# Copying the state-space input out of PSUM in pairs, in another piece order, and turning the second half of a finished block one piece later

## The chip, the cores and the metric

The kernel runs on one core of one Trainium2 chip. The time is the device time of one execution in microseconds. Beside the timed runs there is one profiled execution, whose trace gives every instruction's start and duration.

## The reference

One decoder layer over 256 tokens of width 2048: a SwiGLU feed-forward, a mixer (differential attention beside a state-space branch, S5), and a second SwiGLU feed-forward. Each is fed by an input `u` that is shifted and scaled by a conditioning vector, and each result passes a layer norm. Cut to what matters here:

```
mod = silu(c) @ w_cond + b_cond                       # 9 rows of 2048: shift, scale, gate for three sub-layers
h   = (silu(u @ w1) * (u @ w3)) @ w2                  # feed-forward, inner width 5632
q, k, v, s = split(u @ w_in)                          # mixer: 1024 columns each
attn = diff_attention(q, k, v);  ssm = s5(s)          # s5 scans s over the 256 tokens in 64 groups of 16 channels
h   = concat(attn, ssm) @ w_out
x   = layer_norm(alpha * x + weight * (1 + gate) * h) # after each sub-layer
```

## The kernel before, in words

All weights are read once, as **pieces** of 128 x 1024 numbers (512 KB). `Stream` runs one job for each piece, in the order of a list that Python builds. Around each job it does four things: SP loads the piece into a `raw` buffer, ScalarE casts it to a rounded `hi` (L691), VectorE subtracts to get the rest `lo`, and TensorE multiplies the input (itself split into `Uh` and `Ul`) with `hi` and `lo`. The cast and the subtraction are issued four pieces ahead of the multiplication (`AHEAD`). VectorE also does the conditioning product (`gv`) in between, at places that are fixed when the program is built. Each engine executes its instructions in the order in which the Python code issues them, so the list of jobs and the calls after each job set everything. `stream.later(n, f)` runs `f` after the job that is n pieces later. Nearly every vector and matrix instruction carries line L106, that of a helper, so the rows are told apart by tile names.

**The mixer's s pieces.** `mk_s(t, hf)` multiplies one piece of `w_in`. There are eight tiles `t` of 128 columns of s, and two halves `hf` of the 2048-long sum. Before, the list is all eight tiles with the first half, then all eight with the second. Two neighbouring tiles (t even, t odd) share one PSUM bank (tile `ps`), each using 256 of its 512 columns. After a tile's second half `post` copies its columns to `sT` with ScalarE (L1147) and stores that to a DRAM buffer `sD` by a DMA that ScalarE issues (L1150). After tiles 3 and 7 POOL issues four loads each (L1156) that read `sD` back in the layout of the scan, into `U4` (`U` in the profile). The first matmuls of the scan (`enter` in `s5_batch`, on `U` and `s5e`) stand ahead of job 17 of the mixer, that is behind the sixteen s pieces and one q piece. They need the four loads of tiles 0 to 3.

During the first five s pieces the second half of the mixer's input is still being made: after each of jobs 1 to 4 TensorE turns blocks of `Y`, and ScalarE and VectorE make `Uh` and `Ul` of them. The pieces with hf = 1 need those.

**The k-outer blocks of the feed-forward.** The first blocks of `w1` and `w3` are multiplied in several passes over parts of the inner sum (`mk_ko`). Each block b has two parts, m = 0 (`w1`) and m = 1 (`w3`), and each part holds two PSUM banks. Between passes the partial sums are kept in the SBUF tile `kosum`. In the last pass of the first feed-forward a part is two pieces, so that a block is four. After a part's last piece VectorE adds both banks to `kosum`, which frees the banks. After m = 1, one piece later, `up_post` multiplies silu of the one with the other, and `turn_up` puts two **turnings** on the list: two pieces later TensorE transposes half of the product into one PSUM bank (`ps<-ident,kosum`), ScalarE casts it to `Hh` (L1010) and VectorE makes `Hl`, which frees that bank; one piece after that comes the other half. Four banks are held all through by a block that stays in PSUM, so that only four change hands here. The silu of the next block's m = 0 (L990) falls beside the first turning.

In the second feed-forward, where a part of the last pass is four pieces, the same code runs with b = 1 to 3 (b = 0 takes another path).

Of the kernel before, what the change touches and what calls it, by code (L numbers as in the profile page):

```python
# [17 lines left out]
T = 256  # L18
# [99 lines left out]
def tile_layer(tc, A, out):  # L118
    nc = tc.nc
    V, S, PE, SP, GP = Meter(nc.vector), nc.scalar, Meter(nc.tensor), nc.sync, nc.gpsimd  # L120
    with ExitStack() as ctx:
# [8 lines left out]
        def psum():  # L130
            return psp.tile([128, 512], F32, tag="ps", name="ps")
# [4 lines left out]
        def small(shape, name, bufs=2, dt=F32, tag=None):  # L136
            return tmp.tile(shape, dt, tag=tag or name, name=name, bufs=bufs)

        def w1(shape, name):
            return small(shape, name, 5, tag="w1")  # L140
# [49 lines left out]
        for q in range(4):  # L190
            p, cs = psum(), slice(q % 2 * 512, q % 2 * 512 + 512)
# [9 lines left out]
        sD = dram.tile([1024, 4, 64], F32, tag="sD", name="sD")  # L201
# [530 lines left out]
        stream = Stream()  # L732
# [19 lines left out]
        def between(k):  # L752

            if k in mid:
                mid.pop(k)()
# [22 lines left out]
        def form_b(pd, hi, lo, AH, AL, k0, first, last):  # L778
            for t, p in enumerate(pd):
                if isinstance(p, tuple):  # L780
                    for i in range(2):
                        form_b1(p[i], hi, lo, AH, AL, k0, t, first, last, 256 * i, 256 * i + 256)
                else:
                    form_b1(p, hi, lo, AH, AL, k0, t, first, last)
# [27 lines left out]
        def halves(w, h):  # L812
            return w[:, h * CH:(h + 1) * CH]
# [112 lines left out]
        def ffn(w13, wd, blk, passes, tiles, kept):  # L926
            jobs = []
            B = {}

            def mk_ko(i, b, m, kp):  # L930

                k0, k1 = passes[i]
                keep = 4 * b in kept
                n = len(passes) - 1
                first = i == 0 or not (keep or b == order(i)[0])
                last = i == n or not (keep or b == order(i)[-1])

                def mm(hi, lo):
                    if first and 2 * kp == k0:
                        B["ko", b, m] = [psum(), psum()]  # L940
                    form_b(B["ko", b, m], hi, lo, *st["U"], 2 * kp, first and 2 * kp == k0, last and 2 * kp + 2 == k1)

                def post():
                    if keep or not last:
                        return
                    ps = B.pop(("ko", b, m))
                    if i == n and ("sum", b) not in B:
                        if m == 0:
                            B["s", b] = gated(ps)
                        else:  # L950
                            up_post(B.pop(("s", b)), ps, 4 * b)
                        return
                    if m == 0 and ("sum", b) not in B:
                        B["sum", b] = (pslab if b in ((1, 2) if blk else (3, 4)) else slab)("kosum")
                    a = [B["sum", b][:, (2 * m + t) * 512:(2 * m + t + 1) * 512] for t in range(2)]
                    for t in range(2):
                        if ("added", b, m) not in B:
                            S.copy(a[t], ps[t])
                        else:
                            V.tensor_tensor(a[t], ps[t], a[t], op=ALU.add)  # L960
                    B["added", b, m] = True
                    if i < n:
                        return
                    if m == 0:
                        B["a", b] = a
                        stream.later(1, lambda: gated(a, a))
                        return
                    s = B.pop(("a", b))
                    if b < 4:
                        stream.later(1, lambda: up_post(s, a, 4 * b))  # L970
                    else:
                        stream.later(1, lambda: hold(b, s, a))
                return Job(mm, halves(w13[b, m, kp // 2], kp % 2), post if 2 * kp + 2 == k1 else None)

            def order(i):

                bs = [b for b in range(tiles // 4) if 4 * b not in kept]
                return bs if (len(passes) - 1 - i) % 2 == 0 else bs[::-1]

            def hold(b, s, ps):  # L980

                B["held", b] = [w2([128, 512], "sg") for _ in range(2)]
                for t in range(2):
                    V.tensor_tensor(B["held", b][t], s[t], ps[t], op=ALU.mult)

            def gated(ps, s=None):

                s = s or [w2([128, 512], "sg") for _ in range(2)]
                for t in range(2):
                    S.activation(s[t], ps[t], AF.Silu)  # L990
                return s

            def up_post(s, ps, slot):

                for t in range(2):
                    V.tensor_tensor(s[t], s[t], ps[t], op=ALU.mult)
                turn_up(s, slot)

            def turn_up(s, slot, n=2):
                if slot == 0:  # L1000
                    st["H"] = pairs("H")

                def turned(i):
                    p = psum()
                    for j in range(2):
                        for t in range(2):
                            PE.transpose(p[:, j * T + t * 128:j * T + t * 128 + 128],
                                         s[t][:, (2 * i + j) * 128:(2 * i + j + 1) * 128], ident)
                    hh, hl = (kx(x, slot + 2 * i, 0, 2 * T) for x in st["H"])
                    S.copy(hh, p)  # L1010
                    V.tensor_tensor(hl, p, hh.bitcast(F32), op=ALU.subtract)
                stream.later(n, lambda: turned(0))
                stream.later(n + 1, lambda: turned(1))

            def mk_up(b, m, kp, slot):
                def mm(hi, lo):
# [69 lines left out]
            for i, (k0, k1) in enumerate(passes):  # L1086
                n = len(jobs)
                kps = range(k0 // 2, k1 // 2)
                bs = order(i) + [x // 4 for x in kept[::4]]
                c = (0 if i else 1 if blk else 2)  # L1090
# [4 lines left out]
            for pi, (f0, nf) in enumerate(PIECES):  # L1095
                n = len(jobs)
                for s in range(max(0, min(tiles - f0, nf)), nf, 4):
                    jobs += [mk_up((f0 + s) // 4, m, kp, s) for m in range(2) for kp in range(8)]
                if pi == 1:
                    for s in range(0, tiles - f0, 4):  # L1100
                        b = 4 + s // 4
# [15 lines left out]
        def mixer():  # L1117
            jobs = []
            M = {}
# [10 lines left out]
            def mk_s(t, hf):  # L1130
                def mm(hi, lo):
                    if hf == 0 and t % 2 == 0:
                        M["ps", t // 2] = psum()
                    M["pt"] = p = M["ps", t // 2][:, (t % 2) * T:(t % 2 + 1) * T]
                    for k in range(8):
                        between(8 * hf + k)
                        w = hi[:, k * 128:(k + 1) * 128]
                        PE.matmul(p, w, kx(st["U"][0], 8 * hf + k), start=hf == 0 and k == 0 and t % 2 == 0,
                                  stop=False, skip_group_check=True)
                        PE.matmul(p, w, kx(st["U"][1], 8 * hf + k), start=False, stop=False, skip_group_check=True)  # L1140
                    for k in range(8):
                        PE.matmul(p, lo[:, k * 128:(k + 1) * 128], kx(st["U"][0], 8 * hf + k), start=False,
                                  stop=hf == 1 and k == 7, skip_group_check=True)

                def post():
                    s = w1([128, 4, 64], "sT")
                    S.copy(s, M["pt"].rearrange("p (c i) -> p i c", i=4))  # L1147
                    if t % 2:
                        M.pop(("ps", t // 2))
                    S.dma_start(sD[t * 128:(t + 1) * 128], s)  # L1150
                    if t % 4 == 3:
                        h = t // 4
                        if h == 0:
                            M["U4"] = slab("U4")
                        for i in range(4):
                            GP.dma_start(  # L1156
                                M["U4"][32 * i:32 * i + 32, h * 1024:(h + 1) * 1024]
                                .rearrange("p (g c) -> p g c", c=64),
                                sD[h * 512:(h + 1) * 512, i, :].rearrange("(g p) c -> p g c", p=32))
                return Job(mm, halves(A["win_a"][t], hf), post if hf else None)  # L1160
# [300 lines left out]

            g08 = small([128, 1], "g08", 1)
            V.tensor_scalar(g08, sublng, 1.0 - LAMBDA_INIT, None, op0=ALU.mult)
            jobs += [mk_s(t, hf) for hf in range(2) for t in range(8)]
            for h in range(NH):
                jobs += [mk_qk(h, w, hf) for w in "qk" for hf in range(2)]
            jobs += [mk_v(db, c) for db in range(2) for c in range(8)]
# [79 lines left out]
        for i in range(4 * NT1):  # L1547
            n = ((10, 12, 16, 16)[i] if i < 4 else NS + math.ceil((i - 3) * NS / (GA[0] - 3)) if i <= GA[0] else
                 min(4 * NS, 2 * NS + math.ceil((i - GA[0]) * NS / GA[1])))
# [129 lines left out]
```

## Time and profile before

| what | value |
|---|---|
| timed runs, median of 3 (lowest, highest) | 1914.42 us (1912.57, 1918.12) |
| profiled execution, its own time | 1912.22 us |
| its span, first to last instruction | 1910.4 us |
| mean granted TensorE clock | 0.989 |
| HBM traffic | 278 GB/s over the span |

About 1.8 us lie around the span. Times below count from the span's start. "Idle" before a TensorE instruction, with the name of what released it, is time that TensorE lost; idle of another engine costs nothing by itself.

### The profile page before, as it was taken

Reading aid. Unit: us, or ns where it says so; the run is one execution under the profiler, and the core shown is the slowest. Engines: PE = TensorE matmul, PEld = TensorE weight load, DVE = VectorE, ACT = ScalarE, POOL = GpSimd, SP = SyncE. Lnnn points to the kernel's source line nnn. Section 1 sums busy time; section 2 is a strip of 40 time slices with the busy share of each in tenths; the row PEclk is TensorE's granted clock in tenths of the full one; section 3 lists DMA queues with packets and bytes.
Section 4 is the critical chain, followed back from the end, with each engine's and each line's share of the span. In section 5 each row is a group of like instructions: output and inputs, shape, how many; then the busy total and the mean of one; then the engine's idle time right before and its main releaser. Section 6 shows DMA issues by size and latency. Waiting matters only on the chain.

```text
span 1910.4 us, 25429 instructions
## 1 busy us (share of the span) xinstructions
PE 1858.5 (97%) x9326; PEld 1567.5 (82%) x9326; DVE 1488.1 (78%) x2255; ACT 889.4 (47%) x1211; POOL 65.0 (3%) x119
## 2 busy tenths in 40 slices
PE   6999999999999999899999998999999999999996
PEld 5888878888888888889999886888888888888885
DVE  6889899978888979888998987887876555445468
ACT  3544444465445433634457635544444444344442
POOL 0000000000000000111210000000000000000000
PEclk9999999999999999999999998999999999999998
DMA  9999878889899888798988885998887555565563
GB/s 375 363 338 315 296 247 292 295 306 309 305 347 326 308 323 312 280 337 294 313 268 311 283 309 202 339 357 275 294 279 249 187 188 191 194 215 187 191 233 110
DMA packets 151935, 532.36 MB, mean 279 GB/s; under 512 B 21841, under 2 KB 23297, under 8 KB 150657
## 3 DMA queue, kind: packets, MB, share of 16 engines
q1 hardware_dynamic: 137234, 495.32, 74.3%
q0 software_dynamic: 6512, 23.89, 3.7%
q10 hardware_dynamic: 8064, 11.54, 1.7%
q8 instruction: 73, 1.20, 0.2%
q14 instruction: 52, 0.43, 0.1%
HBM read 513.34 MB, written 17.33 MB: 278 GB/s over the span
## 4 chain that ended last, share of the span: by engine, by line
PE 87%; DVE 6%; DMA 4%; ACT 2%; issue 1%; POOL 0%; SPq 0%; DVEq 0%; ACTq 0%; POOLq 0%
PE ps L106 87%; DVE lo L106 2%; DVE Y L106 2%; DMA raw<-in_f1w_dram 1%; DVE gv L106 1%; ACT hi L691 1%; DMA early<-in_w_cond_dram 1%; DMA raw<-in_wout_dram 0%; DMA U<-sD 0%; DVE st L106 0%; DVE r L106 0%; DMA sD<-sT 0%; DMA early<-in_wc_dram 0%; ACT Y L865 0%; DVE early L106 0%
## 5 line engine op out<-in xcount | busy, mean ns | idle before, releaser
L106 DVE TENSOR_TENSOR lo<-raw,hi 128x1024 fp32r<-128x1024 f32 x630 | 766.3, 1222 | 342.1 <-ACT hi L691 338.5
L691 ACT CAST hi<-raw 128x1024 fp32r<-128x1024 f32 x630 | 661.4, 1053 | 705.8 <-PE ps L106 461.0
L106 PE MATMUL ps<-hi,Uh 128*128 128x512 f32 x1472 | 583.7, 397 | 16.7 <-ACT Uh L318 9.7
L106 PE MATMUL ps<-hi,Ul 128*128 128x512 f32 x1472 | 577.5, 392 | 0.8 <-DVE Ul L106 0.8
L106 PE MATMUL ps<-lo,Uh 128*128 128x512 f32 x1472 | 457.4, 392 | 1.3 <-DVE lo L106 1.3
L106 PEld LDWEIGHTS ps<-hi,Uh 128*128 128x128 f32 x1472 | 278.7, 189 | 77.8 <-ACT Uh L318 10.4
L106 PEld LDWEIGHTS ps<-lo,Uh 128*128 128x128 f32 x1472 | 278.4, 189 | 60.9 <-DVE lo L106 2.0
L106 PEld LDWEIGHTS ps<-hi,Ul 128*128 128x128 f32 x1472 | 279.0, 190 | 58.1 <-DVE Ul L106 1.9
L106 DVE SCALAR_TENSOR_TENSOR gv<-gv,sc 128x1024 f32<-128x1024 f32 x258 | 314.2, 1219 | 1.4 <-DMA gv<-in_w_cond_dram 1.3
L106 PE MATMUL ps<-hi,Hh 128*128 128x512 f32 (+1 forms) x716 | 274.6, 385 | 0.0
L106 PE MATMUL ps<-hi,Hl 128*128 128x512 f32 (+1 forms) x716 | 273.6, 383 | 0.0
L106 PE MATMUL ps<-lo,Hh 128*128 128x512 f32 (+1 forms) x716 | 216.5, 384 | 1.8 <-DVE lo L106 1.8
L106 PEld LDWEIGHTS ps<-lo,Hh 128*128 128x128 f32 x716 | 133.0, 188 | 29.1 <-DVE lo L106 2.6
L106 PEld LDWEIGHTS ps<-hi,Hh 128*128 128x128 f32 x716 | 134.5, 188 | 26.8 <-issue 0.4
L106 PEld LDWEIGHTS ps<-hi,Hl 128*128 128x128 f32 x716 | 134.6, 188 | 26.0
L106 PE MATMUL ps<-Uh,hi 128*128 128x256 f32 x384 | 97.9, 292 | 2.4 <-ACT sT L1147 1.8
L106 PE MATMUL ps<-Ul,hi 128*128 128x256 f32 x384 | 95.7, 286 | 0.1
L106 PEld LDWEIGHTS ps<-Uh,hi 128*128 128x128 f32 x384 | 74.2, 193 | 6.2 <-ACT sT L1147 2.7
L106 PEld LDWEIGHTS ps<-Ul,hi 128*128 128x128 f32 x384 | 74.2, 193 | 0.8 <-DVE Ul L106 0.7
L1010 ACT CAST Hh<-ps 128x512 fp32r<-128x512 f32 x44 | 25.8, 587 | 78.6 <-PE ps L106 78.6
L106 PE MATMUL ps<-Uh,lo 128*128 128x256 f32 x384 | 53.9, 283 | 0.0
L106 DVE TENSOR_TENSOR Hl<-ps,Hh 128x512 fp32r<-128x512 f32 x44 | 30.3, 688 | 30.0 <-ACT Hh L1010 29.7
(229 smaller groups left out, 1393.4 us busy)
## 6 DMA issues: line engine op xcount, KB each, us to landing
raw<-in_f1w_dram SPq DMA_DIRECT2D x264, 512.0 KB, 6.0
raw<-in_f2w_dram SPq DMA_DIRECT2D x264, 512.0 KB, 4.7
gv<-in_w_cond_dram SPq DMA_DIRECT2D x258, 512.0 KB, 7.1
raw<-in_win_a_dram SPq DMA_DIRECT2D x48, 512.0 KB, 6.0
raw<-in_wout_dram SPq DMA_DIRECT2D x32, 512.0 KB, 5.8
early<-in_w_cond_dram SPq DMA_DIRECT2D x28, 512.0 KB, 7.6
s5m<-scrB POOLq DMA_DIRECT2D x8, 1024.0 KB, 8.4
raw<-in_win_v_dram SPq DMA_DIRECT2D x16, 512.0 KB, 4.8
```

What stands on the lines that cost most here:

```text
L106: return f(*a, **k)
L691: S.copy(hi, raw)
L1010: S.copy(hh, p)
```

## The change

It has two parts.

**The s pieces.** The list of jobs becomes tiles 0 to 5 with the first half, tiles 0 to 3 with the second, tiles 6 and 7 with the first, tiles 4 to 7 with the second. An even tile's `post` does nothing; the odd tile's `post` copies both halves of the bank and stores both. The number of copies (8), stores (8) and loads (8) is the same. The loads of tiles 0 to 3 are issued after job 9 where it was job 11, those of tiles 4 to 7 after job 15 as before.

**The second turning.** For b below 3 on the path through `kosum` the second turning runs two pieces after the first, where it was one. That is three blocks of the first feed-forward (b = 0, 1, 2) and two of the second (b = 1, 2).

```
-                        stream.later(1, lambda: up_post(s, a, 4 * b))
+                        stream.later(1, lambda: up_post(s, a, 4 * b, 2 if b < 3 else 1))
...
-            def turn_up(s, slot, n=2):
+            def turn_up(s, slot, n=2, step=1):
...
                 stream.later(n, lambda: turned(0))
-                stream.later(n + 1, lambda: turned(1))
+                stream.later(n + step, lambda: turned(1))
...
                 def post():
-                    s = w1([128, 4, 64], "sT")
-                    S.copy(s, M["pt"].rearrange("p (c i) -> p i c", i=4))
-                    if t % 2:
-                        M.pop(("ps", t // 2))
-                    S.dma_start(sD[t * 128:(t + 1) * 128], s)
+                    if t % 2 == 0:
+                        return
+                    p = M.pop(("ps", t // 2))
+                    for i in range(2):
+                        s = w1([128, 4, 64], "sT")
+                        S.copy(s, p[:, i * T:(i + 1) * T].rearrange("p (c i) -> p i c", i=4))
+                        S.dma_start(sD[(t - 1 + i) * 128:(t + i) * 128], s)
...
-            jobs += [mk_s(t, hf) for hf in range(2) for t in range(8)]
+            jobs += [mk_s(t, hf) for ts, hf in (((0, 1, 2, 3, 4, 5), 0), ((0, 1, 2, 3), 1), ((6, 7), 0), ((4, 5, 6, 7), 1))
+                     for t in ts]
```

On ScalarE, at the mixer's s pieces, this stood in a row before (`ps_6793` is the bank of tiles 0 and 1, `ps_6930` that of tiles 2 and 3; the cast `hi` is that of the piece four ahead):

```order
L1147 COPY sT_7203<-ps_6793 128x256
L1150 DMA sD_128<-sT_7203 128x256
L691 CAST hi_7207<-raw_7063 128x1024
L1147 COPY sT_7246<-ps_6793 128x256
L1150 DMA sD_128<-sT_7246 128x256
L691 CAST hi_7250<-raw_7099 128x1024
L1147 COPY sT_7283<-ps_6930 128x256
L1150 DMA sD_128<-sT_7283 128x256
```

And now:

```order
L1151 COPY sT_7159<-ps_6793 128x256
L1152 DMA sD_128<-sT_7159 128x256
L1151 COPY sT_7162<-ps_6793 128x256
L1152 DMA sD_128<-sT_7162 128x256
L691 CAST hi_7166<-raw_7015 128x1024
L691 CAST hi_7209<-raw_7063 128x1024
L1151 COPY sT_7248<-ps_6930 128x256
L1152 DMA sD_128<-sT_7248 128x256
L1151 COPY sT_7251<-ps_6930 128x256
L1152 DMA sD_128<-sT_7251 128x256
```

Copies and stores come two by two, with two casts between the pairs, and the first pair stands two casts earlier than the second copy of its bank did. On TensorE the piece that follows a pair writes another bank than the one that is being copied, where before the odd tile's piece wrote the bank that the even tile's copy was reading.

On VectorE, in the last pass of the first feed-forward, this stood in a row before (`kosum_856` is block 0, `kosum_584` block 1, `kosum_481` block 2; `ps_2040` and `ps_2041` are block 1's banks for m = 1, `ps_2087` the second turning of block 0, `ps_2103` and `ps_2104` block 2's banks for m = 0):

```order
L106 TENSOR_TENSOR kosum_584<-ps_2040,kosum_584 128x512
L106 TENSOR_TENSOR kosum_584<-ps_2041,kosum_584 128x512
L106 TENSOR_TENSOR Hl_2012<-ps_2087,Hh_2010 128x512
L106 TENSOR_TENSOR lo_2095<-raw_1989,hi_2094 128x1024
L106 SCALAR_TENSOR_TENSOR gv_1944,acc_1892<-gv_1944,sc_74 128x1024
L106 TENSOR_TENSOR kosum_584<-kosum_584 128x512 x2
L106 TENSOR_TENSOR lo_2120<-raw_2018,hi_2119 128x1024
L106 TENSOR_TENSOR kosum_481<-ps_2103,kosum_481 128x512
```

And now (`ps_2110` is the second turning, `ps_2096` and `ps_2097` are block 2's banks):

```order
L106 TENSOR_TENSOR kosum_584<-ps_2040,kosum_584 128x512
L106 TENSOR_TENSOR kosum_584<-ps_2041,kosum_584 128x512
L106 TENSOR_TENSOR lo_2088<-raw_1989,hi_2087 128x1024
L106 SCALAR_TENSOR_TENSOR gv_1944,acc_1892<-gv_1944,sc_74 128x1024
L106 TENSOR_TENSOR Hl_2012<-ps_2110,Hh_2010 128x512
L106 TENSOR_TENSOR kosum_584<-kosum_584 128x512 x2
L106 TENSOR_TENSOR lo_2120<-raw_2018,hi_2119 128x1024
L106 TENSOR_TENSOR kosum_481<-ps_2096,kosum_481 128x512
```

`Hl` of the second turning moves behind one `lo` and one `gv`; nothing else on VectorE moves. On TensorE the four transposes of the second turning move behind the first piece of block 2. By the program's waits, block 2's second bank was the one that the add `kosum_584<-ps_2040` frees; now the second turning takes that bank, and block 2's first piece takes the bank of the first turning and one that the adds of block 1's m = 0 freed.

More of the change, by code (lines that the diff above doesn't have):

```diff
@@ L991, in gated, with up_post @@
                 return s
-            def up_post(s, ps, slot):
+            def up_post(s, ps, slot, step=1):
                 for t in range(2):
                     V.tensor_tensor(s[t], s[t], ps[t], op=ALU.mult)
-                turn_up(s, slot)
-            def turn_up(s, slot, n=2):
+                turn_up(s, slot, 2, step)
+            def turn_up(s, slot, n=2, step=1):
                 if slot == 0:
@@ L1133, in mm @@
                         M["ps", t // 2] = psum()
-                    M["pt"] = p = M["ps", t // 2][:, (t % 2) * T:(t % 2 + 1) * T]
+                    p = M["ps", t // 2][:, (t % 2) * T:(t % 2 + 1) * T]
                     for k in range(8):
```

## The prediction

> **What bounds the kernel now.** First the profile's page: the busy line and the chain that ended last.
>
> ```profile
> PE 1858.5 (97%) x9326; PEld 1567.5 (82%) x9326; DVE 1488.1 (78%) x2255; ACT 889.4 (47%) x1211; POOL 65.0 (3%) x119
> ...
> PE 87%; DVE 6%; DMA 4%; ACT 2%; issue 1%; POOL 0%; SPq 0%; DVEq 0%; ACTq 0%; POOLq 0%
> ```
>
> TensorE (PE) is busy for 97% of the span and holds 87% of the chain. The change takes away no matmul, so it can only win back time in which PE waits. The waits of PE alone, longest first in total (total us, times, longest), name three that lie where the change works:
>
> ```profile
> PE ps L106 <- DVE kosum L106: 3.3, 3, 1.2
> ...
> PE ps L106 <- DMA U<-sD: 2.3, 1, 2.3
> PE ps L106 <- ACT sT L1147: 1.8, 4, 0.5
> ```
>
> Together 7.4 us; the other waits of PE lie elsewhere. Whether time won there reaches the end is read from stretches behind the first and the second place (stretch, its length, then busy us of PE, PEld, DVE, ACT, POOL, granted clock, DMA share, GB/s):
>
> ```profile
> 400.00:460.00 60.00, 60.00 (x315) 49.29 (x318) 48.62 (x73) 33.26 (x59) 3.65 (x6) 1.00 0.88 308
> ...
> 850.00:900.00 50.00, 50.00 (x425) 48.80 (x425) 38.77 (x69) 20.67 (x41) 9.72 (x17) 1.00 0.91 297
> ```
>
> PE is busy without a gap there while VectorE (DVE) has 11 of 60 and 11 of 50 us free. Loads, casts and subtractions follow PE's own progress, since their buffers come free by it. So what PE wins stays won. About 0.3% (5.7 us) is what a measurement of this kernel can tell from no change.
>
> **The copies of s.** ScalarE (ACT) in order of time at the s pieces with hf = 1 (start, duration, what, idle before it); the eight copies run from 820.68 to 843.73:
>
> ```profile
> 820.68 0.37 ACT L1147 COPY sT<-ps 128x256 f32<-128x256 f32 x1 [2.78 <-PE ps L106]
> 821.08 0.33 ACTq L1150 DMA_DIRECT2D sD<-sT  x1
> 821.51 1.06 ACT L691 CAST hi<-raw 128x1024 fp32r<-128x1024 f32 x1 [0.45 <-ACT sT L1147]
> 824.29 0.37 ACT L1147 COPY sT<-ps 128x256 f32<-128x256 f32 x1 [1.72 <-PE ps L106]
> ...
> 827.16 0.37 ACT L1147 COPY sT<-ps 128x256 f32<-128x256 f32 x1 [1.00 <-PE ps L106]
> ...
> 831.17 0.33 ACTq L1150 DMA_DIRECT2D sD<-sT  x1
> ...
> 843.73 0.37 ACT L1147 COPY sT<-ps 128x256 f32<-128x256 f32 x1 [1.73 <-PE ps L106]
> ```
>
> And PE, on the first of four such places:
>
> ```profile
> 821.11 0.39 PE L106 MATMUL ps<-Uh,hi 128*128 128x256 f32 x1 [0.46 <-ACT sT L1147]
> ```
>
> A copy starts when its piece ends. From an even tile's copy to the odd tile's are 3.61 us (820.68 to 824.29), from odd to even 2.87 (824.29 to 827.16). A piece takes 2.87, and the odd tile's piece is held up until the even tile's copy has left the shared bank: 0.74 us, of which 0.46 show as idle and the rest is the last matmul running out. Four times 0.74 is **2.96 us**. After the change no piece follows a copy of its own bank: the next one writes the next pair's. The copies, 2 x 0.83 us with their stores (820.68 to 821.51), then lie beside a piece of 2.87. The cast behind them comes up to 0.83 later, but it is for a piece four ahead, some 11 us; without that cover 4 x 0.83 would fall on PE. I take the whole 2.96. The four waits are the bound above. A bound below zero would need the second half of the input, which job 6 now asks for, to be late:
>
> ```profile
> 810.91 0.76 DVE L106 TENSOR_TENSOR Ul<-uf,Uh 128x256 fp32r<-128x256 f32 x2
> ```
>
> It is complete at 811.67. Job 6 starts 3 pieces before the first copy (820.68 - 3 x 2.87 = 812.07) and uses its last block later still. Nothing waits.
>
> **The scan's input.** PE's one wait for U, and POOL's loads of tiles 0 to 3:
>
> ```profile
> 848.87 1.97 PE L106 MATMUL ps<-U,s5e 128*128 128x64 f32 x16 [2.30 <-DMA U<-sD]
> ```
>
> ```profile
> 838.16 2.59 POOL L1156 DMA_DIRECT2D U<-sD  x4 [46.89 <-ACT sT L1147]
> ```
>
> From tile 3's store (831.17) to the loads' issue are 6.99 us, from there to PE's start 10.71. Tile 3's piece becomes the tenth of the list; in the old trace the tenth ended at 824.29, less one hold-up 823.55. Tile 2's copy and store (0.83) go first, then tile 3's copy, so its store starts at 823.55 + 0.83 + 0.40 = 824.78. Then 824.78 + 6.99 + 10.71 = 842.48. PE is ready at 848.87 - 2.30 - 2.96 = 843.61. U is 1.1 us early and the wait goes: **2.30 us**. The spread of the store and the loads (us to landing, least, median, most) gives the other bound:
>
> ```profile
> DMA to landing us min/median/max: 4.4/6.9/8.9
> ```
>
> ```profile
> DMA to landing us min/median/max: 6.5/7.7/8.6
> ```
>
> With the slowest of each, 2.0 and 0.9 over the median, U comes 1.8 us after PE, and 0.5 us is won.
>
> [...]
>
> **The second turning.** PE in the last pass of the first feed-forward; `ident,kosum` are the turnings:
>
> ```profile
> 251.11 0.60 PE L106 MATMUL ps<-ident,kosum 128*128 128x128 f32 x4
> ...
> 254.28 0.51 PE L106 MATMUL ps<-hi,Uh 128*128 128x512 f32 x1 [1.18 <-DVE kosum L106]
> ...
> 258.50 0.39 PE L106 MATMUL ps<-hi,Uh 128*128 128x512 f32 x1
> ...
> 261.23 0.60 PE L106 MATMUL ps<-ident,kosum 128*128 128x128 f32 x4
> ...
> 264.42 0.60 PE L106 MATMUL ps<-ident,kosum 128*128 128x128 f32 x4
> ...
> 267.49 0.50 PE L106 MATMUL ps<-hi,Uh 128*128 128x512 f32 x1 [1.08 <-DVE kosum L106]
> ```
>
> A piece is 2.73 (258.50 to 261.23), a turning with the piece behind it 3.19 (261.23 to 264.42). A lap of four pieces and two turnings would be 2 x 3.19 + 2 x 2.73 = 11.84. It is 13.21:
>
> ```profile
> 254.28:267.49 13.21, 12.13 (x56) 9.72 (x57) 11.80 (x17) 6.22 (x8) 0.00 (x0) 1.00 0.67 237
> ```
>
> So each of three laps loses 1.37, on the bank that an add frees late. DVE is nearly as full, 11.80 of 13.21. Its rows:
>
> ```profile
> 253.54 1.28 DVE L106 TENSOR_TENSOR kosum<-ps,kosum 128x512 f32<-128x512 f32 x2
> ...
> 259.95 1.28 DVE L106 TENSOR_TENSOR kosum<-ps,kosum 128x512 f32<-128x512 f32 x2
> ...
> 264.46 1.23 DVE L106 TENSOR_TENSOR lo<-raw,hi 128x1024 fp32r<-128x1024 f32 x1 [1.29 <-ACT hi L691]
> 265.60 1.22 DVE L106 SCALAR_TENSOR_TENSOR gv<-gv,sc 128x1024 f32<-128x1024 f32 x1
> 266.75 0.08 DVE L106 DVE_READ_ACCUMULATOR gv<-gv,sc 128x1 f32 x1
> 266.75 1.28 DVE L106 TENSOR_TENSOR kosum<-ps,kosum 128x512 f32<-128x512 f32 x2
> 267.95 0.68 DVE L106 TENSOR_TENSOR Hl<-ps,Hh 128x512 fp32r<-128x512 f32 x1
> ```
>
> Count from the first turning (261.23). The add starts at +5.52 (266.75) and its first half frees the bank at +6.25: before it DVE idles for a cast that ACT makes behind `Hh` and silu of this same turning, so the add hangs on the turning and not on the queue. After the change PE does turning and piece (+3.19), then block 2's first piece at once (+5.92), and only then asks for that bank: a wait of 0.33 where 1.37 was lost. But from that add to the next block's first add DVE works 6.41 without a gap (253.54 to 259.95), and the next first turning needs a bank of that one: +5.52 + 6.41 + 0.73 = +12.66. PE would be there at +6.25 + 3.19 + 2.73 = +12.17. So the lap becomes 12.66 and no shorter, 0.54 less than 13.20 (DVE's idle 1.29 shrinks to 0.75, so the add still hangs on the turning). Three laps: **1.62 us**. Bounds: 3 x 1.37 = 4.1 if neither wait appears; nothing if DVE fills the lap again; a loss is the last rival below. I take 1.62, since both waits follow from rows of this stretch.
>
> In the second feed-forward PE does not wait at these places. Rows of PE, DVE and SP there:
>
> ```profile
> 1353.07 0.60 PE L106 MATMUL ps<-ident,kosum 128*128 128x128 f32 x4
> ```
>
> ```profile
> 1353.20 1.28 DVE L106 TENSOR_TENSOR kosum<-ps,kosum 128x512 f32<-128x512 f32 x2
> ```
>
> ```profile
> 1362.67 0.42 SPq L880 DMA_DIRECT2D bb<-in_lnb_dram  x1
> ```
>
> The second turning moves one piece, to 1355.8; the add has freed a bank by then, 1353.9. SP's load of `bb` takes over the slab that this turning reads, and SP's weight loads stand behind it, but it is issued 7 us later. Zero, either way.
>
> **The sum.** 2.96 + 2.30 + 1.62 = 6.88. The profiled execution took 1912.22, so it would take 1905.3. The median of the runs shown is 1914.42, 2.2 above it; the median is what is compared, so I predict 1914.42 - 6.88 = 1907.5.
>
> **The rivals.**
> - *The laps lose nothing any more* (-4.1 there, 9.4 in all: 1905.1). For it: DVE can work only 11.80 in a lap. Against: the two bank waits above.
> - *The laps win nothing*: DVE stays the bound and the wait only moves from a matmul to a turning (-5.26: 1909.2). For it: DVE has no gap but one. Against: that gap can shrink.
> - *The wait for U stays in part* (0.5 of 2.30 won, 5.1 in all: 1909.3; not won at all, 1909.8). For it: only 1.1 us of margin under landings that spread over 4.5. Against: both medians.
> - *The s part does not do what it says* and PE still waits for copies (-1.62: 1912.8). Against: by the program's waits a piece behind a pair waits for its weights alone.
> - *Slower*: on ACT the cast `Hh` of the second turning now stands behind one more cast of weights. When that piece's load is late, `Hh` is late, then `Hl`, and behind `Hl` DVE's whole queue, on which PE's banks hang. Loads can be late: ACT's waits for them in the first feed-forward (total, times, longest) are
>
> ```profile
> ACT hi L691 <- DMA raw<-in_f1w_dram: 127.5, 75, 6.2
> ```
>
> `Hl` would end at +5.52 + 1.28 + 1.23 + 1.22 + 0.68 = +9.93, and PE needs its bank in the second half of the piece behind +9.44, at about +10.8, so it decides from 0.9 us of lateness on. With the longest wait a lap loses 5.3, three laps 15.9, less the 5.26 of the mixer: 10.6 slower, 1925.1. Against: in the rows of this stretch DMA has a share of 0.67, and no cast there waits for a load.
>
> **How the numbers follow.** Chances: forecast 0.48; laps lose nothing 0.14; laps win nothing 0.18; U's wait stays 0.13; no effect of the s part 0.03; slower 0.04. The range reaches from the best case less the 2 us by which runs fall below their median (1912.57 against 1914.42), 1903.0, to the case of U with as much on top, 1911.5. The cases at 1909.2 to 1909.8 lie just inside 0.3% (1908.7 is the line) and the forecast 1.2 us outside it, so each gives a part to the other side: faster 0.75 x 0.48 + 0.14 + 0.3 x 0.18 + 0.2 x 0.13 = 0.58; slower 0.04; the rest, 0.38, within.
>
> **What would show it.** In the profile after: no wait of PE for `sT`, none for U; matmul waits for `kosum` replaced by waits of about 0.3 to 0.5 us of the turnings; the laps at 12.7; the first matmuls on U at about 843.6 less what the laps won, 842.0. Wrong would be: a wait for U over 1 us, laps still at 13.2 or at 11.9, or a new wait for `Uh` or `Ul` at job 6.

## The result and the profile after

The changed kernel took 1905.26 us (median of 6 runs, 1903.30 to 1908.48), the kernel before 1915.37 beside it (median of 6, 1910.42 to 1920.72). The ratio is 0.9946, with a 95% interval of 0.9927 to 0.9964. That is about 10 us faster, where 6.9 were forecast. A second comparison on another occasion gave 1905.53 against 1914.18, a ratio of 0.9951 (0.9939 to 0.9964). The profiled execution of the changed kernel took 1903.43, with a span of 1901.6.

The page's busy line and its chain:

```profile
PE 1855.7 (98%) x9326; PEld 1566.4 (82%) x9326; DVE 1487.8 (78%) x2255; ACT 889.5 (47%) x1211; POOL 65.3 (3%) x119
...
PE 89%; DVE 6%; DMA 3%; ACT 1%; issue 1%; SPq 0%; DVEq 0%; ACTq 0%
```

PE is still the bound, with 89% of the chain, where it had 87%. Of the waits of PE (total us, times, longest), these three are in the middle of the list:

```profile
...
PE ps L106 <- DVE lo L106: 2.2, 2, 1.4
PE ps L106 <- DVE kosum L106: 1.5, 6, 0.3
PE ps L106 <- DVE Uh L106: 1.1, 2, 0.6
...
```

The rows for `sT` and for `U` are gone from this view. The three long waits for `kosum` have become six short ones. ScalarE's copies of s, in order of time:

```profile
815.48 0.37 ACT L1151 COPY sT<-ps 128x256 f32<-128x256 f32 x1 [1.90 <-PE ps L106]
815.88 0.33 ACTq L1152 DMA_DIRECT2D sD<-sT  x1
816.25 0.37 ACT L1151 COPY sT<-ps 128x256 f32<-128x256 f32 x1 [0.40 <-DVE Y L106]
...
821.24 0.37 ACT L1151 COPY sT<-ps 128x256 f32<-128x256 f32 x1 [1.16 <-PE ps L106]
...
823.08 0.33 ACTq L1152 DMA_DIRECT2D sD<-sT  x1
```

The two copies of a pair lie 0.77 apart, and the pairs 5.76, which is two pieces without a hold-up. Tile 3's store goes out at 823.08. The first matmuls on `U`, the first row without a wait:

```profile
841.50 1.97 PE L106 MATMUL ps<-U,s5e 128*128 128x64 f32 x16
```

In the laps PE now waits at the turnings, and a lap takes 12.74 (PE rows of a second turning and of the next first turning, then the lap as a stretch with busy us of PE, PEld, DVE, ACT, POOL, granted clock, DMA share, GB/s):

```profile
254.31 0.66 PE L106 MATMUL ps<-ident,kosum 128*128 128x128 f32 x4 [0.31 <-DVE kosum L106]
260.72 0.66 PE L106 MATMUL ps<-ident,kosum 128*128 128x128 f32 x4 [0.28 <-DVE kosum L106]
```

```profile
254.31:267.05 12.74, 12.27 (x57) 9.64 (x57) 11.72 (x17) 6.11 (x8) 0.00 (x0) 1.00 0.71 245
```

Each kernel has three profiles in the end (two more of each are among the experiments), so the gain can be split by stage. A stage runs from the start of one row of PE to that of another: the first turning, the wait for `s5w` near 400, the first wait for `Y` (near 786, and near 1145), the first matmul on `U`, the last matmul.

| stage, us | before, three profiles | after, three profiles | mean difference |
|---|---|---|---|
| start to first turning | 247.88, 250.43, 250.53 | 247.90, 248.74, 249.13 | -1.0 |
| first turning to `s5w` (the laps) | 152.03, 152.09, 152.02 | 150.69, 150.65, 150.69 | -1.37 |
| `s5w` to first `Y` | 386.80, 385.65, 385.91 | 385.78, 387.42, 385.54 | +0.1 |
| first `Y` to first matmul on `U` (the s pieces) | 62.16, 63.11, 62.39 | 57.13, 57.45, 57.70 | -5.13 |
| first matmul on `U` to second `Y` | 302.44, 304.49, 302.93 | 301.38, 301.58, 302.88 | -1.34 |
| second `Y` to last matmul | 744.33, 744.34, 743.23 | 744.11, 744.11, 744.25 | +0.2 |

The laps and the s pieces came out as worked out (1.62 and 5.26). What was not forecast is the 1.34 behind the first matmul on `U`, and 1.0 at the start, where the change touches nothing and single runs differ by 2.6.

### The profile page after: what moved, and what is told of

Same layout as the page of the kernel before. It is cut to its first block, busy times and chain, and to the rows that moved or that the text cites. A ratio compares the mean times of both kernels' runs of the same rounds, so it can differ in the third digit from the quotient of the medians.

```text
span 1901.6 us, 25429 instructions
## 1 busy us (share of the span) xinstructions
PE 1855.7 (98%) x9326; PEld 1566.4 (82%) x9326; DVE 1487.8 (78%) x2255; ACT 889.5 (47%) x1211; POOL 65.3 (3%) x119
## 4 chain that ended last, share of the span: by engine, by line
PE 89%; DVE 6%; DMA 3%; ACT 1%; issue 1%; SPq 0%; DVEq 0%; ACTq 0%
PE ps L106 89%; DVE lo L106 2%; DVE Y L106 1%; DVE gv L106 1%; DMA raw<-in_f1w_dram 1%; DMA raw<-in_f2w_dram 1%; DVE kosum L106 1%; DMA early<-in_w_cond_dram 1%; ACT hi L691 0%; DVE st L106 0%; DVE r L106 0%; DMA early<-in_wc_dram 0%; DMA gv<-in_w_cond_dram 0%; ACT Y L865 0%; ACT uf L743 0%
```

## The experiments

**The two halves of the change apart.** The s edits alone keep `turn_up`'s second turning one piece behind the first; the turning alone keeps the old `mk_s` and list:

```
s_alone:       stream.later(1, lambda: up_post(s, a, 4 * b, 1))
turning_alone: old post() of mk_s, old list of the sixteen s pieces
```

> Both edits of s alone (pairs and new order of the pieces), the second turning one piece behind the first as before. Theory (the parts are separate: 2.96 us of hold-ups and 2.30 us of the wait for U go): PE has no wait for sT and none for U, the laps stay at 13.2 with three waits of about 1.1 for kosum, the first matmul on U comes 5.3 us after-less-before earlier, and the time is 5.3 us under before. Rival (the copies were hidden, and only U's wait was paid): 2.3 us under before. Rival on the end of the first feed-forward (the 1.20 us wait for lo at 773.97 that the changed kernel no longer has was removed by the turning's edit): that wait is there in this run.

> The edit of the second turning alone, the copies of s and their order as before. Theory: the laps go from 13.2 to 12.74, 1.4 us in all; PE still waits four times about 0.46 for sT and once for U, 2 to 3 us; the time is 1.4 us under before, which is within what the timing can tell from no change. Rival (the edit also takes away the waits for lo at the ends of the first feed-forward and of the mixer, 1.20 and 0.60): those are gone in this run and the time is 3.2 us under before. Other rival (those waits come and go with the loads and have nothing to do with the edit): they may be there or not in any run.

Measured: s alone 1906.57 against 1916.17, ratio 0.9953 (0.9941 to 0.9965), 9.0 us (6.7 to 11.3). The turning alone 1914.75, ratio 0.9996 (0.9987 to 1.0004), 0.8 us. The parts add up to the whole within these intervals (9.8 of 10). The laps' stage is 152.01 with s alone and 150.65 with the turning alone, so the 1.4 us belong to the turning and are too small for the timing. But s alone wins more than the 5.3 that were expected, though PE still waits 0.36 for `U` there. Of the waits for `lo`, neither run has the one near 774.

**Pairs and order apart.** One kernel copies in pairs but keeps the old list, the other keeps single copies in the new list (both with the old turning):

```
pairs_in_old_order:      jobs += [mk_s(t, hf) for hf in range(2) for t in range(8)]
new_order_single_copies: old post() of mk_s, new list
```

> The copies in pairs, but the pieces in the old order (all eight first halves, then all eight second halves), turning as before. Theory (tile 3's store now starts behind the twelfth piece, at about 830.5 on the old clock, so U is ready 17.7 later, at 848.2, while PE, without the hold-ups, is there at 843.6): no wait for sT, one wait for U of 4.6 us instead of 2.3, and only 0.65 us under before. Rival (the pairs alone carry the gain, and U comes as early as PE): 5 us under before, wait for U under 1 us.

> The new order of the pieces, but each tile copied out behind its own piece as before, turning as before. Theory: four waits for sT of about 0.46 (2.96 us of hold-ups) stay; tile 3's store starts at about 825.4, U is ready at 843.1 and PE is there at 846.6, so the wait for U goes: 2.3 us under before. Rival (the hold-ups are worth nothing, the order carries the whole gain): 5.3 us under before.

Pairs in the old order: 1915.12, ratio 0.9997 (0.9987 to 1.0007). Its only wait of the two kinds:

```profile
PE ps L106 <- DMA U<-sD: 4.9, 1, 4.9
```

So it is as the theory had it: the hold-ups go, PE is earlier, and all of that is lost again at `U`, which is not earlier. New order with single copies: 1908.51, ratio 0.9966 (0.9953 to 0.9979), 6.5 us (4.0 to 9.0), where 2.3 were expected. Its trace has the four waits that the theory keeps:

```profile
PE ps L106 <- ACT sT L1147: 1.8, 4, 0.5
```

There is no row for `U`. Hence taking away the wait for `U` must be worth more than the 2.3 us that the first profile of before shows. The rows behind the wait say why. This is the kernel with the pairs in the old order, from the first matmul on `U` to the scan's next ones, and as much behind that:

```profile
846.23:863.47 17.24, 17.24 (x112) 17.24 (x113) 8.79 (x14) 4.44 (x6) 3.13 (x5) 0.75 1.00 328
863.47:880.00 16.53, 16.53 (x143) 16.13 (x142) 11.94 (x21) 4.32 (x7) 3.29 (x6) 1.00 0.75 253
```

The same stretch in the first profile of before, where the wait was 2.30:

```profile
848.87:862.23 13.36, 13.36 (x112) 13.36 (x113) 8.47 (x14) 4.44 (x6) 3.13 (x5) 1.00 1.03 344
```

The same 112 matmuls take 17.24 instead of 13.36, at a granted clock of 0.75 instead of 1.00. Row by row it is a clock of a half for a while, and then a full one again:

```profile
846.23 3.65 PE L106 MATMUL ps<-U,s5e 128*128 128x64 f32 x16 [4.89 <-DMA U<-sD]
...
852.77 0.41 PE L106 MATMUL ps<-Uh,hi 128*128 128x256 f32 x1
...
854.84 0.28 PE L106 MATMUL ps<-Uh,hi 128*128 128x256 f32 x1
```

Sixteen matmuls take 3.65 where the changed kernel takes 1.97, and a matmul of 0.28 takes 0.41. This wait of PE cost its length and, behind it, a slow clock: 3.9 us more.

**Is it the idleness, and how long was before's wait as a rule?** Four runs: the kernel before twice more; the pairs in the old order with the scan a piece later, so that the wait is shorter; and the same kernel with useless matmuls in the wait.

```
pairs_old_order_scan_later:   -S5_AT = 17
                              +S5_AT = 18
pairs_old_order_filled, in enter(), b == 0, ahead of the matmuls on U:
    u, now = st["U"][0], PE.t
    for k in range(34):
        PE.matmul(p[:, 0:256], kx(u, k % 16, 0, 128), kx(u, k % 16), start=True, stop=True)
    ...
```

> The kernel before once more, one profile. [...] No wait for lo near 774. Rival: the wait for U is 2.3 in each run, and the runs differ elsewhere.

> As the run ahead of it, a further profile of the kernel before, with the same expectations.

> Pairs in the old order (the kernel of the earlier run), with the scan's eight batches each one piece later. [...] Rival (a wait costs its own length and the low clock is a thing of that run): 2.9 us under, about 1912.

> Pairs in the old order, and PE does 34 matmuls more (128x256 each, of Uh with itself, into the bank that the scan's first matmuls then overwrite) ahead of the first matmul on U: about 34 x 0.12 = 4.1 us of idle work inside the wait of 4.9. Theory (the low clock behind the wait comes from PE's idleness): what is left of the wait is about 0.8, the sixteen matmuls on U take 1.97, the clock stays 1.00, and from the first of them to the wait for Y near 1150 are 301.4 to 301.9 us instead of 305.3; 3.4 us under the kernel without the filling. Rival (the low clock comes of the time that passes or of the run, not of the idleness): sixteen matmuls of 3.6 and 305 us as before, and no gain.

Before once more took 1916.68 and 1913.58. The wait for `U`, in the one and in the other:

```profile
851.28 3.29 PE L106 MATMUL ps<-U,s5e 128*128 128x64 f32 x16 [3.38 <-DMA U<-sD]
```

```profile
850.85 2.57 PE L106 MATMUL ps<-U,s5e 128*128 128x64 f32 x16 [2.65 <-DMA U<-sD]
```

And behind it in the first of the two:

```profile
851.28:867.76 16.48, 16.48 (x113) 16.48 (x113) 7.40 (x13) 4.45 (x6) 3.13 (x5) 0.79 0.92 302
```

That is 3.1 us more than 13.36; in the second it is 14.91, 1.55 more, behind a wait of 2.65, with a granted clock of 0.70 from 850 to 855 and 0.96 from 855 to 860. So the profile on which the forecast rested showed the kernel before at its best: the wait was 2.30 with a full clock behind it, where the three profiles together give 2.8 us of wait and 1.6 of slow clock.

The filled kernel says, in its one profile, that it is the idleness. PE works through the time and finds `U` ready:

```profile
845.52 4.24 PE L106 MATMUL ps<-Uh 128*128 128x256 f32 x34
849.78 1.97 PE L106 MATMUL ps<-U,s5e 128*128 128x64 f32 x16
```

```profile
849.78:863.15 13.37, 13.37 (x112) 13.37 (x113) 9.05 (x14) 4.45 (x6) 3.13 (x5) 1.00 1.04 330
```

The stretch is back at 13.37 at a clock of 1.00, and from there to the second `Y` are 301.39 instead of 305.26, as expected. The 3.4 us that were expected did not show in the time: 1912.24 against 1914.18, ratio 0.9994 (0.9983 to 1.0005), where 0.9997 (0.9987 to 1.0007) was measured without the filling. That is 0.6 us between the two, and the intervals only just leave room for 3.4. The mean granted clock, which every run has, is finer: 0.9905 over 11 runs with the filling (0.9903 for the kernel before beside it), 0.9885 over 12 runs without (0.9894). By the difference of these differences, 0.001 of 1910 us, the filling saves some 2 us of slow clock in the mean, which is an estimate. A single profile of each doesn't say how often the clock falls, so the mean price stays open.

The other waits of PE speak for the idleness too. In stretches of 5 us, from 20 to 1885 us, the granted clock in the first profile of before and in that of after is under 0.97 only beside waits of PE: between 35 and 50, between 780 and 795 and between 1140 and 1170. The first wait for `Y`, which the change doesn't touch, is 3.06 in both and followed by a slow clock in both (0.65 before and 0.50 after, from 785 to 790). In the changed kernel:

```profile
784.37 1.11 PE L106 MATMUL ps<-ident,Y 128*128 128x128 f32 x4 [3.06 <-DVE Y L106]
```

```profile
785.00:790.00 5.00, 4.42 (x20) 3.80 (x18) 4.60 (x11) 4.18 (x9) 2.21 (x5) 0.50 0.96 341
```

The scan a piece later won nothing: 1915.19, ratio 1.0001 (0.9992 to 1.0011), where the rival had about 1912. The wait became 2.66 and the clock fell nonetheless (0.64 and 0.68 in the two stretches of 5 us behind 850). Besides, the shifted batches of the scan met other waits, two of 2.5 in all for `s5e`. So a wait that went from 4.89 to 2.66 was still followed by a slow clock.

**What sets the lap.** The changed kernel, with VectorE's background work left out in the three laps and made up later, once all of it and once one `gv` of the two in a lap:

```
laps_without_gv, in drain():  if st["lim"] is None or 74 <= stream.done <= 90:
                                  return
  and at the top of the file: GVM = (0.63, 0.65, 0.85, 0.4)
laps_one_gv_less, in drain(): if 77 <= stream.done <= 90:
                                  if stream.done in (79, 83, 87):
                                      gv_step()
                                  return
                              ...
                              st["gv_credit"] += stream.done in (100, 104, 108)
```

> The changed kernel, with no background work of VectorE (no gv, no cells) in the three laps; what is left out there is done later in the same stage (rate 0.63 instead of 0.57). Theory (a lap is set by DVE's unbroken 6.42 us from add to add and the one gv ahead of the add: two gv of 1.14 less, 4.4 + 5.3 + 0.7 = 10.4 against PE's 12.2): no wait for kosum is left in the laps, a lap takes 11.84 instead of 12.74, 2.7 us in three, about 1903 if the rest stays. Rival (the add hangs on ScalarE's cast, not on DVE's work): laps stay at 12.7. Other rival (the gv put off make the rest of the stage late): laps at 11.84 but the time as the changed kernel's or over it.

> The changed kernel with one of the two gv of each lap left out there (and the few cells), the three made up one by one some 20 to 30 pieces later. Theory (the lap of 12.74 is DVE's chain, and 1.14 off it makes 11.6, under PE's own 11.84): the laps take 11.84 as with both gv gone, no wait for kosum; and with only 3 x 1.22 us put off, the end of the stage isn't late as it was with all put off: 2.7 us under the changed kernel, about 1902.5. Rival (DVE is full in the whole stage and whatever is put off comes back): laps at 11.84 and the same time as the changed kernel.

Without `gv` a lap has no wait left:

```profile
255.84:267.69 11.85, 11.85 (x57) 9.79 (x56) 9.61 (x13) 6.11 (x8) 0.00 (x0) 1.00 0.51 178
```

That is 11.85 where 11.84 was worked out from a piece and a turning. With one of the two left in, a lap is 12.24 (257.01 to 269.25):

```profile
257.01 0.66 PE L106 MATMUL ps<-ident,kosum 128*128 128x128 f32 x4 [0.19 <-DVE kosum L106]
262.98 0.60 PE L106 MATMUL ps<-ident,kosum 128*128 128x128 f32 x4
269.25 0.66 PE L106 MATMUL ps<-ident,kosum 128*128 128x128 f32 x4 [0.18 <-DVE kosum L106]
```

The wait at the second turning stays, the one at the next first turning is gone. 11.84 was expected here; the `gv` that was left in is the one ahead of the add, on which the second turning hangs. The one behind it was worth 0.5 a lap, the one ahead 0.4. DVE's work sets the lap, as the forecast had it.

The times: 1907.03, ratio 0.9939 (0.9926 to 0.9953), and 1905.69, ratio 0.9951 (0.9938 to 0.9965), not to be told from the changed kernel's 0.9946 and 0.9951. What the laps win is paid back before the first wait for `Y`: from the first turning to there the two take 540.1 and 537.5, where the three profiles of the changed kernel have 536.2 to 538.1. In the first of the two the work put off shows at the end of the stage:

```profile
775.67 0.73 PE L106 MATMUL ps<-lo,Hh 128*128 128x512 f32 x2 [3.32 <-DVE lo L106]
```

In the second it is a wait of 2.2 for `sg` near 677, where the changed kernel has 0.7, and the clock is 0.53 from 679 to 682 behind it. No version that was tried beats the changed kernel.

**The changed kernel twice more.**

> The changed kernel once more. Theory (it wins 2.96 + 1.4, and of U's wait 2.8 in the mean with 1.3 of slow clock behind it, 8.5 in all): no wait for U or under 1 us, clock 1.00 behind it, laps at 12.74, 8 to 9 us under the kernel before. The wait for lo near 774 may be there or not. Rival (the wait for lo at the end of the first feed-forward is gone because of the change): never a wait for lo near 774, here and in the further run.

> As the run ahead of it, one more profile, with the same expectations.

1905.53, ratio 0.9951, and 1906.65. In the first, PE waits for `lo` at the end of the first feed-forward:

```profile
774.05 0.74 PE L106 MATMUL ps<-lo,Hh 128*128 128x512 f32 x2 [1.67 <-DVE lo L106]
```

The first profile of before has 1.20 there, the other two none, the first of after none. The wait comes and goes in both kernels and is no part of the change. In the second run PE waits 1.02 for `U`, and the clock falls even so:

```profile
843.06 1.97 PE L106 MATMUL ps<-U,s5e 128*128 128x64 f32 x16 [1.02 <-DMA U<-sD]
844.84 0.36 PE L106 MATMUL ps<-Uh,hi 128*128 128x256 f32 x1
...
845.34 0.42 PE L106 MATMUL ps<-Ul,hi 128*128 128x256 f32 x1
```

```profile
843.06:857.93 14.87, 14.87 (x112) 14.87 (x113) 11.42 (x16) 6.91 (x10) 3.13 (x5) 0.89 1.01 334
```

## Why the prediction was right, and where it was not

**The bound.** Right but for the clock. The forecast said that the change can only win back time in which PE waits; of the 8.5 us between the profiles some 1.05 are time in which PE worked at a slow clock. Nothing is given back later beyond +0.1 and +0.2 in the stages behind the laps and behind the mixer.

**The copies of s, 2.96.** Right. No wait for `sT`, and the s pieces' stage is shorter by 5.13 in the mean, of which 2.3 are the wait for `U` (2.8 before, 0.5 after); 2.9 are left for the hold-ups. With single copies in the new order the four waits of 0.46 are all there. No wait for `Uh` or `Ul` appeared at job 6. On ScalarE the last pair is copied late, at 841.28 where the piece had long ended, since casts stand in front of it; nobody waits for it.

**The scan's input, 2.30.** The mechanism was right, its size too small. The first matmuls on `U` came at 841.50, forecast 842.0. The chain to POOL's loads held:

```profile
829.56 2.58 POOL L1158 DMA_DIRECT2D U<-sD  x4 [40.98 <-DMA sD<-sT]
```

That is 45.2 behind PE's first wait for `Y`, and 45.4 and 45.5 in the other two profiles; the forecast was 831.77 - 786.71 = 45.06. From the loads' issue to PE's start the forecast took the 10.71 of one row. The other profiles of before have 11.0 and 12.3, and those of after, where PE waits, 12.0 and 12.2. So `U` isn't 1.1 us early but between about in time and 1.0 late. The late loads cost little, since before waited for such loads too: the wait fell from 2.8 to 0.5 in the mean, by 2.3. That this is the 2.30 of the forecast is luck, because both ends were off by 0.5. What failed is the price of the wait: "The wait goes: 2.30 us" takes a wait at its length. The wait in that profile was the shortest of the three, and no slow clock stood behind it; behind the two longer ones there was one. In the mean of three profiles the slow clock cost 1.6 us before and 0.5 after, so taking the wait away was worth 2.3 + 1.05.

**The second turning, 1.62.** Right in mechanism, 1.37 in the result. The two waits are where they were put: 0.33 forecast at the second turning, 0.2 to 0.3 measured, and 0.49 (12.66 - 12.17) forecast at the next first turning, 0.28 measured. The idle of these rows is not the whole loss: a lap is 0.89 longer than PE's own 11.85, and 0.47 of it (0.19 + 0.28) shows as idle. The lap is 12.74 and not 12.66. VectorE's rows of the changed kernel, behind the first turning at 260.72:

```profile
264.02 1.23 DVE L106 TENSOR_TENSOR lo<-raw,hi 128x1024 fp32r<-128x1024 f32 x1 [1.02 <-ACT hi L691]
...
266.30 1.29 DVE L106 TENSOR_TENSOR kosum<-ps,kosum 128x512 f32<-128x512 f32 x2
...
272.72 1.28 DVE L106 TENSOR_TENSOR kosum<-ps,kosum 128x512 f32<-128x512 f32 x2
```

The add starts 5.58 behind the turning (forecast 5.52), the next add 6.42 behind it without a gap (6.41), and the turning that needs its bank 0.74 behind that start (0.73). DVE still idles 1.02 ahead of `lo`, where 0.75 was forecast. Taking away DVE's work shortens the lap to PE's own 11.85, so it was this chain. The rival in which the laps win nothing is out, and so is the one in which they lose nothing.

**The second feed-forward, 0.** Right: the stage from the second `Y` to the last matmul took 744.0 before and 744.2 after.

**The sum.** From 6.88: 0.25 less in the laps, 0.13 less at the s pieces and 1.34 behind them that were in no term make 7.84. The stages of the three profiles add up to 8.5 in the mean, 1.0 of it at the start, and their whole times differ by 8.7. The medians differ by 10.1 and 8.7, with intervals of 7 and 5 us. The rest is not resolved.

**The rivals.** The wait for `U` staying in part came true in two of three profiles, at 0.5 and 1.0, but the forecast compared it with a wait of 2.30 that was itself too short. The slow rival, `Hh` behind a late cast, appeared in no profile: the laps are 12.74 in each.

## What to carry to other kernels

A wait that depends on a transfer is a spread and not a number (2.30, 3.38 and 2.65 for `U` in three profiles of the kernel before): take it from several profiles, and look at the granted clock of the stretch behind it before pricing it (13.36 us at 1.00 behind the first, 16.48 at 0.79 behind the second). A consumer that was made faster won nothing alone where it then waited for its producer (pairs alone: ratio 0.9997, a wait of 4.9), while the producer that was moved earlier won 6.5 us alone (the new order with single copies). Work that was moved off a chain on an engine that is full elsewhere in the stage was paid back there (laps of 11.85 instead of 12.74, and 540.1 us up to the wait for `Y` instead of 536.2 to 538.1).

## What the runs showed of the hardware

The granted clock fell behind waits for `U` of 2.65 (0.70 from 850 to 855), 2.66 (0.64 from 850 to 855), 3.38 (0.67 from 850 to 855) and 4.89 us (0.50 from 847 to 850) and behind one of 1.02 (0.72 from 843 to 848), and not behind 0.49 (1.00 from 843 to 848) and 2.30 (1.00 from 848.87 to 862.23). So no length of the wait alone decides. Elsewhere it fell behind a wait of 2.20 for `sg` (with one `gv` less in the laps; matmuls of 128x512 take 0.63 there, from 679.54 on), and not behind 1.67 for `lo` (the changed kernel once more; they take 0.40 right behind it). In the longest wait for `U`, from 841.34 to 846.23, it fell while PE stood still: it is 1.00 from 838 to 843 and 0.69 from 843 to 847, of which PE works only from 846.23 on. With that wait filled it is 1.00 in each stretch from 838 to 865. In the case of 1.02 the fall begins only behind the sixteen matmuls of 64 columns, in the rows from 844.84 to 845.34; behind the wait of 2.30 the same sixteen were followed by no fall. What decides between the two was not shown.
